# An average-pooling kernel that streams 134 MB through VectorE: merged output stores, one store kept back to the end, and a finer tail

## The chip, the cores and the metric

The kernel runs on one core of a Trainium2 chip. The metric is device time in microseconds (us), lower is better. Executions of one kernel mostly agree within about 0.3%, so the median of several is quoted. The "span" of a profile is the time from the first to the last instruction of the profiled execution; it is about 2 us shorter than the device time of the same execution.

## The reference

The input `x` has the shape 32 x 256 x 4096 in float32 (134 MB). Every 16 neighbouring values of a row are averaged, so the output is 32 x 256 x 256 (8.4 MB).

```python
def reference(x, output_size):          # output_size = 256
    for i in range(output_size):
        start = int(i * length / output_size)
        end = int((i + 1) * length / output_size)
        result[:, :, i] = np.mean(x[:, :, start:end], axis=-1)
    return result
```

## The kernel before

The whole input is one flat run, cut into tiles of 128 partitions x W columns. For each tile there is one load (issued from SyncE), one reduce over 16 columns on VectorE, one multiply by 1/16 on ScalarE, and one store (issued from ScalarE). There are 24 tiles of 8192 columns (4 MB, one contiguous row of 32 KB per partition), then ten of 4096 and twelve of 2048, so that little work is left after the last load.

```python
    tail = [4096] * 10 + [2048] * 12
    segs = [FULL] * nfull + tail                     # FULL = 8192, nfull = 24
    # ... cut ...
    loads = ctx.enter_context(tc.tile_pool(name="loads", bufs=5))
    outs = ctx.enter_context(tc.tile_pool(name="outs", bufs=10))
    for j, W in enumerate(segs):
        Wo = W // K                                  # K = 16
        # ... cut: x_tile [P, W] from loads, o_tile [P, Wo] from outs ...
        nc.sync.dma_start(out=x_tile,
            in_=xs[xoff:xoff + P * W].rearrange("(p w) -> p w", p=P))
        nc.vector.reduce_sum(out=o_tile,
            in_=x_tile.rearrange("p (o k) -> p o k", k=K), axis=mybir.AxisListType.X)
        nc.scalar.mul(out=o_tile, in_=o_tile, mul=inv_k)
        nc.scalar.dma_start(
            out=os[ooff:ooff + P * Wo].rearrange("(p w) -> p w", p=P), in_=o_tile)
```

Of the kernel before, what the change touches and what calls it, by code (L numbers as in the profile page):

```python
# [1 line left out]

# [4 lines left out]


@with_exitstack
def kernel(  # L10
    ctx: ExitStack,
    tc: tile.TileContext,
    x: bass.AP,
    output_size: int,
    out: bass.AP,
):
    nc = tc.nc
    fp32 = mybir.dt.float32

    B, C, L = x.shape  # L20
    Bo, Co, O = out.shape
    assert B == Bo and C == Co and O == output_size
    assert L % O == 0
    K = L // O

    P = nc.NUM_PARTITIONS

    total_cols = (B * C * L) // P
    FULL = 8192

    tail = [4096] * 10 + [2048] * 12
    nfull = (total_cols - sum(tail)) // FULL
    assert nfull * FULL + sum(tail) == total_cols
    segs = [FULL] * nfull + tail

    xs = x.rearrange("b c l -> (b c l)")
    os = out.rearrange("b c o -> (b c o)")

    inv_k = 1.0 / K

    loads = ctx.enter_context(tc.tile_pool(name="loads", bufs=5))
    outs = ctx.enter_context(tc.tile_pool(name="outs", bufs=10))

    xoff = 0
    ooff = 0
    for j, W in enumerate(segs):
        Wo = W // K
        x_tile = loads.tile([P, W], fp32, tag="x", padded_shape=[P, FULL])
        o_tile = outs.tile([P, Wo], fp32, tag="o", padded_shape=[P, FULL // K])
        nc.sync.dma_start(  # L50
            out=x_tile,
            in_=xs[xoff:xoff + P * W].rearrange("(p w) -> p w", p=P),
        )
        nc.vector.reduce_sum(  # L54
            out=o_tile,
            in_=x_tile.rearrange("p (o k) -> p o k", k=K),
            axis=mybir.AxisListType.X,
        )
        nc.scalar.mul(out=o_tile, in_=o_tile, mul=inv_k)  # L59
        nc.scalar.dma_start(  # L60
            out=os[ooff:ooff + P * Wo].rearrange("(p w) -> p w", p=P),
            in_=o_tile,
        )
        xoff += P * W
        ooff += P * Wo


# [1 line left out]
_INS = ['x', 'output_size']  # L69
_OUTS = [((32, 256, 256), 'float32')]  # L70
#: Inputs that are plain numbers.
_NUMBERS = {'output_size': 256}


# [26 lines left out]
```

## Time and profile before

| | before |
|---|---|
| time, median | 341.87 us (4 runs; 341.77 over 12) |
| span of the profiled run | 340.0 us |
| load packets on the 16 DMA engines (a packet is one row that one engine moves) | 1.76 to 334.30 us |
| last store packet ends | 338.60 us |
| VectorE busy | 279.4 us, 82% |

In all profile lines DVE is VectorE, ACT ScalarE, SP SyncE; SPq and ACTq are their DMA-issuing instructions; L54 is a line of the kernel. These are lines of the profile page of the kernel before: the DMA engines' busy tenths and the rate in 40 slices of the span, the two DMA queues (loads on q1, stores on q10), the chain that ended last, and the reduce.

```profile
span 340.0 us, 355 instructions
DMA  7999999999999999999999999999999999999993
GB/s 312 440 432 447 425 423 459 394 462 406 442 447 405 459 397 459 431 417 459 397 459 405 444 447 405 463 394 455 435 407 434 423 427 434 425 416 420 421 420 135
...
q1 hardware_dynamic: 6624, 134.22, 91.9%
q10 hardware_dynamic: 6624, 8.39, 6.7%
...
DMA 92%; DVE 5%; issue 1%; ACT 0%; SPq 0%; DVEq 0%
...
L54 DVE TENSOR_REDUCE o_tile<-x_tile 128x512 f32<-128x8192 f32 (+2 forms) x46 | 279.4, 6087 | 57.6 <-DMA x_tile<-in_x_dram 55.1
...
out_dram<-o_tile ACTq DMA_DIRECT2D x24, 256.0 KB, 15.0
```

The DMA engines are full from the second slice to the last but one, and the chain is nearly all load. VectorE has 60 us to spare.

The timeline of the end shows the chain: the last reduce, its multiply, its store (start us, duration us, engine, line, operation).

```profile
334.75 2.29 DVE L54 TENSOR_REDUCE o_tile<-x_tile 128x128 f32<-128x2048 f32 x1 [0.34 <-ACT o_tile L59]
337.07 0.31 ACT L59 ACTIVATE o_tile<-o_tile 128x128 f32<-128x128 f32 x1 [2.32 <-DVE o_tile L54]
337.41 0.34 ACTq L60 DMA_DIRECT2D out_dram<-o_tile  x1
```

### The profile page before, as it was taken

The page shows a single profiled execution, that of the slowest core. Times are in us where ns is not written, and L with a number is a line of the kernel's source. Part 1 is how long each engine was busy: PE and PEld are TensorE (multiplying, and loading weights), DVE is VectorE, ACT ScalarE, POOL GpSimd, SP SyncE. Part 2 cuts the span into 40 slices and gives each one's busy share as a digit, 9 for nine tenths or more (in the row PEclk, how much of TensorE's full clock was granted, in tenths as well). Part 3 has the DMA queues.
Part 4 walks back from the last instruction along what each step waited for, and adds up shares of the span by engine and source line. Part 5 has one row for each costly group of instructions (what it writes and reads, how often), then busy time and mean ns, then how long its engine had stood idle before and what let it go on. Part 6 is the DMA issues. An engine that isn't in the chain of part 4 may idle for free.

```text
span 340.0 us, 355 instructions
## 1 busy us (share of the span) xinstructions
DVE 279.4 (82%) x46; ACT 24.3 (7%) x47; POOL 0.2 (0%) x4
## 2 busy tenths in 40 slices
DVE  0488898888988788988888988889889998899885
ACT  1000000000000000000000000000001000001111
POOL 0000000000000000000000000000000000000000
DMA  7999999999999999999999999999999999999993
GB/s 312 440 432 447 425 423 459 394 462 406 442 447 405 459 397 459 431 417 459 397 459 405 444 447 405 463 394 455 435 407 434 423 427 434 425 416 420 421 420 135
DMA packets 13251, 142.64 MB, mean 420 GB/s; under 512 B 1472, under 2 KB 4288, under 8 KB 7360
## 3 DMA queue, kind: packets, MB, share of 16 engines
q1 hardware_dynamic: 6624, 134.22, 91.9%
q10 hardware_dynamic: 6624, 8.39, 6.7%
q14 instruction: 3, 0.02, 0.0%
HBM read 134.22 MB, written 8.39 MB: 419 GB/s over the span
## 4 chain that ended last, share of the span: by engine, by line
DMA 92%; DVE 5%; issue 1%; ACT 0%; SPq 0%; DVEq 0%
DMA x_tile<-in_x_dram 89%; DVE o_tile L54 5%; DMA out_dram<-o_tile 3%; ACT o_tile L59 0%; SPq L50 0%; DVEq L54 0%
## 5 line engine op out<-in xcount | busy, mean ns | idle before, releaser
L54 DVE TENSOR_REDUCE o_tile<-x_tile 128x512 f32<-128x8192 f32 (+2 forms) x46 | 279.4, 6087 | 57.6 <-DMA x_tile<-in_x_dram 55.1
L59 ACT ACTIVATE o_tile<-o_tile 128x512 f32<-128x512 f32 (+2 forms) x46 | 23.0, 500 | 312.4 <-DVE o_tile L54 307.8
L59 ACT ACT_TABLE_LOAD x1 | 1.3, 1283 | 0.7 <-PEq L82 0.7
L82 POOL MEMSET const-bfloat16-1.0<- 128x1 bf16 x1 | 0.1, 102 | 0.0
L82 POOL MEMSET const-uint8-127<- 128x1 uint8 x1 | 0.1, 101 | 0.0
L82 POOL MEMSET const-float32-0.0<- 128x1 f32 x1 | 0.1, 99 | 0.2 <-issue 0.2
L82 POOL MEMSET const-float32-1.0<- 128x1 f32 x1 | 0.1, 98 | 0.0
## 6 DMA issues: line engine op xcount, KB each, us to landing
x_tile<-in_x_dram SPq DMA_DIRECT2D x24, 4096.0 KB, 41.2
x_tile<-in_x_dram SPq DMA_DIRECT2D x10, 2048.0 KB, 20.4
x_tile<-in_x_dram SPq DMA_DIRECT2D x12, 1024.0 KB, 10.4
out_dram<-o_tile ACTq DMA_DIRECT2D x24, 256.0 KB, 15.0
out_dram<-o_tile ACTq DMA_DIRECT2D x10, 128.0 KB, 11.6
out_dram<-o_tile ACTq DMA_DIRECT2D x12, 64.0 KB, 8.2
```

The costliest lines, as they stand in the source:

```text
L54: nc.vector.reduce_sum(out=o_tile, in_=x_tile.rearrange("p (o k) -> p o k", k=K), axis=mybir.AxisListType.X,)
L59: nc.scalar.mul(out=o_tile, in_=o_tile, mul=inv_k)
L82: nc = _bacc.Bacc("TRN2", target_bir_lowering=False, num_devices=1)
```

## The change

The intent is to store in fewer, larger DMAs, issued later (eight tiles after the last tile of a group), and to shorten what is left after the last load. Four or five neighbouring tiles share one output tile and one store (three and one at the very end); the group of the last four full tiles is "deferred": its 1 MB store is issued from SyncE after the last load. The tail ends in four tiles of 1024 columns with load buffers of their own, and the last multiply is done by VectorE. There are four big load buffers in place of five.

```diff
-    tail = [4096] * 10 + [2048] * 12
+    tail = [(10, 4096, 5), (10, 2048, 5), (4, 1024, 3)]    # tiles, columns, tiles per store
+    plan = [(nfull, FULL, 4)] + tail
 ... (cut: the list of groups)
+    STORE_DELAY = 8
+    defer_first_segs = {nfull - 4}
+    for gi, gr in enumerate(groups):
+        last = gr["segs"][-1]
+        if gr["segs"][0] in defer_first_segs and gr["W"] == FULL:
+            gr["kind"] = "defer"
+        elif gi == final_group:
+            gr["kind"] = "final"
+        elif last + STORE_DELAY >= nseg_total:
+            gr["kind"] = "late"
+        else:
+            gr["kind"] = "sync"
+            gr["store_at"] = last + STORE_DELAY
-    loads = ctx.enter_context(tc.tile_pool(name="loads", bufs=5))
-    outs = ctx.enter_context(tc.tile_pool(name="outs", bufs=10))
+    loads = ctx.enter_context(tc.tile_pool(name="loads", bufs=4))
+    outs = ctx.enter_context(tc.tile_pool(name="outs", bufs=4))
+    small = ctx.enter_context(tc.tile_pool(name="small", bufs=4))
+    keep = ctx.enter_context(tc.tile_pool(name="keep", bufs=max(1, len(defer_first_segs))))
 ... (cut: views of a group in HBM, "(s p w) -> p s w", and in its output tile)
-        nc.scalar.mul(out=o_tile, in_=o_tile, mul=inv_k)
-        nc.scalar.dma_start(out=os[...], in_=o_tile)
+        if not final_seg:
+            nc.scalar.mul(...)                             # on the tile's slice of the group
+        else:
+            nc.vector.tensor_scalar_mul(...)
+            nc.scalar.dma_start(out=hbm_ap(gi), in_=sbuf_ap(gi))
+        if gr["kind"] == "late" and s == gr["segs"][-1]:
+            nc.scalar.dma_start(out=hbm_ap(gi), in_=sbuf_ap(gi))
+        for gi2 in stores_at.get(s, []):
+            nc.scalar.dma_start(out=hbm_ap(gi2), in_=sbuf_ap(gi2))
+    for gi, gr in enumerate(groups):
+        if gr["kind"] == "defer":
+            nc.sync.dma_start(out=hbm_ap(gi), in_=sbuf_ap(gi))
```

More of the change, by code (lines that the diff above doesn't have):

```diff
@@ L29 @@
     FULL = 8192
-    tail = [4096] * 10 + [2048] * 12
-    nfull = (total_cols - sum(tail)) // FULL
-    assert nfull * FULL + sum(tail) == total_cols
-    segs = [FULL] * nfull + tail
+    tail = [(10, 4096, 5), (10, 2048, 5), (4, 1024, 3)]
+    tail_cols = sum(n * w for n, w, _ in tail)
+    nfull = (total_cols - tail_cols) // FULL
+    assert nfull * FULL + tail_cols == total_cols
+    plan = [(nfull, FULL, 4)] + tail
     xs = x.rearrange("b c l -> (b c l)")
@@ L39 @@
     inv_k = 1.0 / K
-    loads = ctx.enter_context(tc.tile_pool(name="loads", bufs=5))
-    outs = ctx.enter_context(tc.tile_pool(name="outs", bufs=10))
-    xoff = 0
+    seg_w = []
+    for (nseg, W, G) in plan:
+        seg_w += [W] * nseg
+    nseg_total = len(seg_w)
+    seg_xoff = []
+    off = 0
+    for W in seg_w:
+        seg_xoff.append(off)
+        off += P * W
+    groups = []
     ooff = 0
-    for j, W in enumerate(segs):
+    seg = 0
+    for (nseg, W, G) in plan:
         Wo = W // K
-        x_tile = loads.tile([P, W], fp32, tag="x", padded_shape=[P, FULL])
-        o_tile = outs.tile([P, Wo], fp32, tag="o", padded_shape=[P, FULL // K])
+        for j0 in range(0, nseg, G):
+            g = min(G, nseg - j0)
+            groups.append({
+                "W": W, "Wo": Wo, "og": ooff + j0 * P * Wo,
+                "segs": list(range(seg, seg + g)),
+            })
+            seg += g
+        ooff += nseg * P * Wo
@@ new lines @@
+    group_of_seg = {}
+    j_in_group = {}
+    for gi, gr in enumerate(groups):
+        for k, s in enumerate(gr["segs"]):
+            group_of_seg[s] = gi
+            j_in_group[s] = k
+    final_group = len(groups) - 1
+    assert len(groups[final_group]["segs"]) == 1
+    STORE_DELAY = 8
[11 more added lines that the diff above has]
+            gr["store_at"] = last + STORE_DELAY
@@ new lines, with hbm_ap @@
+    stores_at = {}
+    for gi, gr in enumerate(groups):
+        if gr["kind"] == "sync":
+            stores_at.setdefault(gr["store_at"], []).append(gi)
+    loads = ctx.enter_context(tc.tile_pool(name="loads", bufs=4))
+    outs = ctx.enter_context(tc.tile_pool(name="outs", bufs=4))
+    small = ctx.enter_context(tc.tile_pool(name="small", bufs=4))
+    keep = ctx.enter_context(tc.tile_pool(name="keep", bufs=max(1, len(defer_first_segs))))
+    group_tiles = {}
+    def hbm_ap(gi, lo=0, hi=None):
+        gr = groups[gi]
+        Wo = gr["Wo"]
+        g = len(gr["segs"])
+        if hi is None:
+            hi = g
+        n = hi - lo
+        base = gr["og"] + lo * P * Wo
+        if n == 1:
+            return os[base:base + P * Wo].rearrange("(p w) -> p w", p=P)
+        return os[base:base + n * P * Wo].rearrange("(s p w) -> p s w", p=P, w=Wo)
@@ new lines, in sbuf_ap @@
+    def sbuf_ap(gi, lo=0, hi=None):
+        gr = groups[gi]
+        Wo = gr["Wo"]
+        g = len(gr["segs"])
+        if hi is None:
+            hi = g
+        t = group_tiles[gi][:, lo * Wo:hi * Wo]
+        if hi - lo == 1:
+            return t
+        return t.rearrange("p (s w) -> p s w", w=Wo)
+    for s in range(nseg_total):
+        W = seg_w[s]
+        Wo = W // K
+        gi = group_of_seg[s]
+        gr = groups[gi]
+        j = j_in_group[s]
+        g = len(gr["segs"])
+        final_seg = s == nseg_total - 1
+        if j == 0:
+            pool = keep if gr["kind"] == "defer" else outs
+            tag = "keep" if gr["kind"] == "defer" else "o"
+            group_tiles[gi] = pool.tile([P, g * Wo], fp32, tag=tag, name="ot",
+                                        padded_shape=[P, 4 * (FULL // K)])
+        o_tile = group_tiles[gi]
+        if W == 1024:
+            x_tile = small.tile([P, W], fp32, tag="xs")
+        else:
+            x_tile = loads.tile([P, W], fp32, tag="x", padded_shape=[P, FULL])
@@ L50 @@
         nc.sync.dma_start(
             out=x_tile,
-            in_=xs[xoff:xoff + P * W].rearrange("(p w) -> p w", p=P),
+            in_=xs[seg_xoff[s]:seg_xoff[s] + P * W].rearrange("(p w) -> p w", p=P),
         )
         nc.vector.reduce_sum(
-            out=o_tile,
+            out=o_tile[:, j * Wo:(j + 1) * Wo],
             in_=x_tile.rearrange("p (o k) -> p o k", k=K),
@@ L58 @@
         )
-        nc.scalar.mul(out=o_tile, in_=o_tile, mul=inv_k)
-        nc.scalar.dma_start(
-            out=os[ooff:ooff + P * Wo].rearrange("(p w) -> p w", p=P),
-            in_=o_tile,
-        )
-        xoff += P * W
-        ooff += P * Wo
+        if not final_seg:
+            nc.scalar.mul(
+                out=o_tile[:, j * Wo:(j + 1) * Wo],
+                in_=o_tile[:, j * Wo:(j + 1) * Wo],
+                mul=inv_k,
+            )
+        else:
+            nc.vector.tensor_scalar_mul(
+                out=o_tile[:, j * Wo:(j + 1) * Wo],
+                in0=o_tile[:, j * Wo:(j + 1) * Wo],
+                scalar1=inv_k,
+            )
+            nc.scalar.dma_start(out=hbm_ap(gi), in_=sbuf_ap(gi))
[3 more added lines that the diff above has]
+            nc.scalar.dma_start(out=hbm_ap(gi2), in_=sbuf_ap(gi2))
+    for gi, gr in enumerate(groups):
+        if gr["kind"] == "defer":
+            nc.sync.dma_start(out=hbm_ap(gi), in_=sbuf_ap(gi))
 _INS = ['x', 'output_size']
```

## The prediction

> **What bounds the kernel now.** The 16 DMA engines. The page's DMA row shows nine tenths or more in all but the end slices; the queue table gives loads 91.9% and stores 6.7% of 16 engines' span of 340.0 us. The chain of waits is 89% load, 5% reduce, 3% store. VectorE is busy 82% and waits 55.1 us for loads.
>
> The trace's packet records cost a packet by its size alone: loads 1213 ns (32 KB), 611 (16 KB), 309 (8 KB); stores 84 ns (2 KB), 46 (1 KB), 27 (512 B); completion writes 9 ns. Summed over 16 engines: 335.3 us, between the first load packet at 1.8 us and the last store packet at 338.6. A 32 KB packet in 1213 ns is 432 GB/s over 16 engines, at the 435 GB/s fabric ceiling that the Trainium skill states ("DMA: Bandwidth & Descriptors", Specifications). So only 1.5 us of engine time is idle, nearly all of it after the last load packet (334.3): reduce 2.29, multiply 0.31, store issue and data about 1.6, then 1.35 to the end.
>
> **What the change does.** Loads: same bytes; 2 of the 2048-column loads become 4 of 1024. At an estimated 159 ns per 4 KB packet, +0.1 us. Stores: the merged store of 4 or 5 tiles keeps the same contiguous runs (2 KB, 1 KB, 512 B), so the same packets, +0.15 us for the 256 B ones, and some 31 fewer completion writes, -0.3 us. DMA work stays about 335.3 us.
>
> The gain is in the tail alone: the 1 MB store kept back (32 packets x 84 ns = 2.7 us per engine) and late stores fill the DMA time while the last tile is reduced. That tile's reduce halves to about 1.2 us (estimate from 2.29) and its multiply moves to VectorE. The last load should land about 2.5 us earlier (332), and then about 5.3 us of stores remain.
>
> **What it costs.** Stores alternate with load packets one for one: the first store's packets are 1.30 us apart (1213 + 84), as the skill says of round-robin by packet (same page, "Queues, rings and completion order"). A merged store of 32 packets should thus take four loads, about 43 us, instead of 15. Consequences: (a) the first reduce of the fifth store group waits about 3 us for its output buffer, harmless; (b) loads and stores share eight completion semaphores in turn (seen in the trace), so a load can be held back by a store eight issues earlier; 2 to 3 loads are still queued then, so at most 1 to 2 us near the end; (c) the last reduce reuses the buffer of a 640 KB store that ends about when the last load does, so it waits some 2 us in the tail. Four load buffers instead of five: a load is issued when a reduce ends, with over two loads (20 us) still queued.
>
> **Prediction.** Span 338.7 us, time 340.5 us: -0.4%, within 2%. Range 338.8 to 343.5.
>
> **What would show it.** Total packet time unchanged within 1 us; store issue-to-landing about 40 us for merged stores; last load landing near 332; store queue busy after it for 4 to 6 us; the last reduce waiting for a store, not for its load; no DMA slice below nine tenths in mid-run.
>
> **What would make it wrong.** Upward: semaphore sharing or an output buffer starving loads for several us (a dip in mid-run), or stores piling up after the last load. Downward: merged rows move as larger packets, saving up to about 8 ns of each of some 5,900 store packets, 3 us per engine (estimate from 84 against 46 ns).
>
> Chances: faster by over 2% 0.02, within 2% 0.93, slower by over 2% 0.05.

## More of the kernel before

Where a run is shown by windows, the columns are the window, its length, busy time of VectorE, ScalarE and GpSimd, a clock that doesn't matter here, the mean busy share of the 16 DMA engines, and GB/s.

```profile
15.00:250.00 235.00, 197.76 (x24) 14.47 (x23) 0.00 (x0) 1.00 1.00 430
250.00:300.00 50.00, 46.54 (x10) 3.96 (x9) 0.00 (x0) 1.00 1.01 428
300.00:330.00 30.00, 26.76 (x12) 3.62 (x11) 0.00 (x0) 1.00 1.02 419
...
334.30:338.60 4.30, 2.40 (x2) 0.62 (x2) 0.00 (x0) 1.00 0.12 33
338.60:340.00 1.40, 0.00 (x0) 0.00 (x0) 0.00 (x0) 1.00 0.00 0
```

Two things are to be seen. First, the busy share goes over 1.00, so packet records overlap: those up to the last load packet add up to 334.8 us per engine in a stretch of 332.5 us. Second, between the last load packet (334.30) and the last store packet (338.60) the DMA engines are only 12% busy. Of those 4.30 us, 0.88 x 4.30 = 3.8 us are idle.

## The result, and the profile after

| | before | change |
|---|---|---|
| time, median | 341.77 us (12 runs, 341.54 to 342.16) | 338.32 us (9 runs, 338.13 to 339.53) |
| ratio | | 0.9902, 95% interval 0.9892 to 0.9911 |
| span, profiled run | 340.0 us | 337.7 us, the slowest of the nine |
| span, the other eight | | 336.3 to 336.8 us |

A ratio is the mean time of one kernel's fast runs over that of the other's fast runs of the same rounds, so it is not quite the ratio of the medians quoted. The change is 1.0% faster, 3.45 us, where I predicted 0.4% (about 1.4 us); 338.32 us lies just below my range of 338.8 to 343.5.

The profile page of the change (the profiled run was one of its rare slow ones, see below) answers the lines shown of before: span, DMA busy tenths, queues, chain, and the merged stores with their size and the time from issue to landing.

```profile
span 337.7 us, 266 instructions
DMA  8999999999999999999999999999999999999997
...
q1 hardware_dynamic: 7440, 135.27, 93.5%
q10 hardware_dynamic: 5808, 7.34, 6.0%
...
DMA 77%; DVE 20%; issue 2%; ACT 0%; SPq 0%; DVEq 0%
...
out_dram<-ot ACTq DMA_DIRECT2D x5, 1024.0 KB, 42.2
...
out_dram<-ot SPq DMA_DIRECT2D x1, 1024.0 KB, 6.6
```

The packets are as many in sum (13251 before, 13250 after), and the middle of the run has the same rate. The merged 1 MB stores took 42.2 us to land instead of 15.0, as predicted. SyncE does wait for stores before it issues some loads (7 times, 63.5 us in sum; 6 times and 51.5 us before), but other loads are queued then and no slice of mid-run falls below nine tenths. The last slice went from 3 to 7 tenths: the gain is in the tail.

The change (run again2): a usual execution. Its windows are to be laid beside those of before.

```profile
15.00:250.00 235.00, 199.89 (x24) 14.47 (x23) 0.00 (x0) 1.00 1.00 431
250.00:300.00 50.00, 47.28 (x11) 4.38 (x10) 0.00 (x0) 1.00 1.01 428
300.00:328.00 28.00, 24.85 (x11) 3.20 (x10) 0.00 (x0) 1.00 1.02 419
...
331.20:335.20 4.00, 2.07 (x3) 0.26 (x1) 0.00 (x0) 1.00 0.94 315
335.20:336.60 1.40, 0.00 (x0) 0.00 (x0) 0.00 (x0) 1.00 0.00 0
```

The first three rows differ by at most 1 GB/s from those of before. The last load packet now ends at 331.17 instead of 334.30, and the 4 us after it, in which the last tile is still reduced and stored, are 94% busy instead of 12%. The gain in span is 340.0 - 336.6 = 3.4 us: the last load ends 3.1 us earlier, and the stretch after it is 0.3 us shorter.

One part of the change does nothing at all. These lines of the timeline of the change show the fourth multiply and the first merged store.

```profile
50.83 0.63 ACT L154 ACTIVATE ot<-ot 128x512 f32<-128x512 f32 x1 [9.08 <-DVE ot L148]
51.49 0.42 ACTq L171 DMA_DIRECT2D out_dram<-ot  x1
```

The store goes out as soon as its group is complete, not eight tiles later: the framework's scheduler sets the order, not the place in the source. I built the kernel with delays of 0, 1 and 8 tiles as well and compared the instruction order of every engine: it is the same in all three, so there was nothing to run. (The three programs differ in the numbers of buffer names alone.) So "issued later" must not enter any explanation of the result, and it had entered my prediction.

### The profile page after: what moved, and what is told of

Read it like the earlier page. It is cut to its first block, busy times and chain, and to the rows that moved or that the text cites. A ratio compares the mean times of both kernels' runs of the same rounds, so it can differ in the third digit from the quotient of the medians.

```text
span 337.7 us, 266 instructions
## 1 busy us (share of the span) xinstructions
DVE 279.4 (83%) x49; ACT 24.4 (7%) x48; POOL 0.2 (0%) x4
## 2 busy tenths in 40 slices
DMA packets 13250, 142.63 MB, mean 422 GB/s; under 512 B 1472, under 2 KB 4032, under 8 KB 7616
## 4 chain that ended last, share of the span: by engine, by line
DMA 77%; DVE 20%; issue 2%; ACT 0%; SPq 0%; DVEq 0%
DMA x_tile<-in_x_dram 48%; DMA out_dram<-ot 29%; DVE ot L148 20%; ACT ot L154 0%; SPq L144 0%; DVE ot L160 0%; DVEq L148 0%
## 5 line engine op out<-in xcount | busy, mean ns | idle before, releaser
L148 DVE TENSOR_REDUCE ot<-x_tile 128x512 f32<-128x8192 f32 (+3 forms) x48 | 279.2, 5839 | 55.7 <-DMA x_tile<-in_x_dram 55.7
L154 ACT ACTIVATE ot<-ot 128x512 f32<-128x512 f32 (+3 forms) x47 | 23.1, 492 | 306.9 <-DVE ot L148 306.9
## 6 DMA issues: line engine op xcount, KB each, us to landing
out_dram<-ot ACTq DMA_DIRECT2D x5, 1024.0 KB, 42.2
```

What stands on the lines that cost most here:

```text
L148: nc.vector.reduce_sum(out=o_tile[:, j * Wo:(j + 1) * Wo], in_=x_tile.rearrange("p (o k) -> p o k", k=K), axis=mybir.AxisListType.X,)
L154: nc.scalar.mul(out=o_tile[:, j * Wo:(j + 1) * Wo], in_=o_tile[:, j * Wo:(j + 1) * Wo], mul=inv_k,)
```

## The experiments

Three theories were to be told apart. Theory 1: the gain is idle DMA time after the last load, filled by the kept-back store. Theory 2: the merging of the stores saves DMA or issue time. Theory 3: the shorter chain after the last load (smaller last tile, multiply on VectorE). All times of one round are beside runs of the kernel before on the same chip: 341.82 us in the first round (9 runs), 341.75 in the second (11), 341.83 in the third (9). All outputs were correct.

### b_keep4: only the kept-back store

The kernel before, and nothing else of the change:

```diff
+        held = nfull - 4 <= j < nfull
+        o_tile = kept[:, k0:k0 + Wo] if held else outs.tile(...)
 ...
-        nc.scalar.dma_start(out=os[...], in_=o_tile)
+        if not held:
+            nc.scalar.dma_start(out=os[...], in_=o_tile)
 ... after the loop
+    nc.sync.dma_start(out=os[...].rearrange("(s p w) -> p s w", p=P, w=Wk),
+                      in_=kept.rearrange("p (s w) -> p s w", w=Wk))
```

> The kernel before, with one part of the change alone: the outputs of the last four full tiles are kept back and stored in one 1 MB store after the last load, on the load queue; every other store as it was. Theory 1 (idle tail): before, the DMA engines are idle for about 3.9 us after the last load packet (334.3 us), which my prediction missed because the packet records overlap by 1 to 2%; 32 packets x 84 ns = 2.7 us of store work moved there make the last load land about 2.6 us earlier (near 331.7) and the run about 2.5 us shorter: 339.3 us. Theory 2 (merging): only one merged store here, so nearly nothing is gained: 341.5 us. Theory 3 (shorter tail chain): the chain after the last load is as before: 341.8 us.

Measured: 339.10 us (338.95 to 339.19), ratio 0.992 (0.9906 to 0.9933); span 337.2 us. The windows of the end:

```profile
328.00:331.60 3.60, 3.27 (x2) 0.31 (x1) 0.00 (x0) 1.00 0.99 398
331.60:336.00 4.40, 2.47 (x2) 0.62 (x2) 0.00 (x0) 1.00 0.70 253
```

The last load packet ends at 331.64, which is 2.66 us earlier than before; the work moved is 32 packets x 84 ns = 2.69 us. The stretch after it is as long as before but 70% busy. This one edit gives 2.7 us of the 3.45. Theory 1 holds, with its number. The kept-back store is also merged and stands on SyncE's queue behind the loads; keeping it back on ScalarE's queue was not tried.

### b_tail: only the finer tail

```diff
-    tail = [4096] * 10 + [2048] * 12
+    tail = [4096] * 10 + [2048] * 10 + [1024] * 4
 ...
-        nc.scalar.mul(out=o_tile, in_=o_tile, mul=inv_k)
+        if j < len(segs) - 1:
+            nc.scalar.mul(out=o_tile, in_=o_tile, mul=inv_k)
+        else:
+            nc.vector.tensor_scalar_mul(out=o_tile, in0=o_tile, scalar1=inv_k)
```

> The kernel before, with the tail of the change alone: two of the 2048-column tiles become four of 1024, and the last multiply is on VectorE. DMA work is the same. Theory 3 (shorter tail chain): from the last load packet to the end it was 5.7 us before and 4.5 us in the profile of the change, so about 1.1 us are gained: 340.7 us. Theories 1 and 2 as the only cause: 341.8 us.

Measured: 341.54 us (341.50 to 341.86), ratio 0.9994 (0.998 to 1.0008): nothing clear of noise. The windows of its end, and the last store and load in its chain of waits:

```profile
332.50:334.00 1.50, 1.50 (x3) 0.26 (x1) 0.00 (x0) 1.00 0.78 279
...
335.60:339.80 4.20, 1.42 (x2) 0.00 (x0) 0.00 (x0) 1.00 0.09 19
```

```profile
324.27 7.11 DMA out_dram<-o_tile
...
331.46 3.74 DMA x_tile<-in_x_dram
```

The stretch after the last load did shrink, from 5.7 to 4.2 us. But the last load packet ends at 335.55 instead of 334.30, since the last load was issued only at 331.46, when a store that had been issued at 324.27 had landed; the DMA engines ran partly dry (0.78) meanwhile. In the trace, loads and stores take eight completion semaphores (counters by which a DMA reports that it has landed) in turn, and a DMA may be issued only when the one eight places before it has landed. Halving the tiles halves the work that eight DMAs hold in flight. So a finer tail by itself is paid for with a late last load. The small tiles' own load buffers, which this run lacks and the change has, are not the wait seen here: the semaphores are.

### b_merge: only the merged stores and the four load buffers

The change with its tail, kept-back store and last multiply put back to those of before:

```diff
-    tail = [(10, 4096, 5), (10, 2048, 5), (4, 1024, 3)]
+    tail = [(10, 4096, 5), (11, 2048, 5), (1, 2048, 1)]
-    defer_first_segs = {nfull - 4}
+    defer_first_segs = set()
-            nc.vector.tensor_scalar_mul(...)
+            nc.scalar.mul(...)
```

> The kernel before, with the merging and delaying of the stores and the four load buffers of the change, but nothing kept back and the tail tiles as before. Theory 2 (fewer, larger stores save DMA time or issue time): faster by 2 us or more, 339.5 us. Theories 1 and 3: packets are the same, so 341.8 us within 0.5; if anything slower, as the late stores pile up after the last load.

Measured: 341.07 us (340.84 to 341.50), ratio 0.9981 (0.9969 to 0.9994): 0.75 us faster. Theory 2 as the main cause is out (it wanted 2 us or more), and my 341.8 was a little too high. The last load packet ends 0.55 us earlier than before (333.75). Fewer completion writes (34 DMAs less, 9 ns each on every engine) would account for 0.3 us of it; the rest I did not trace further. Merging and four load buffers were changed together here, so only their sum is known to do no harm.

### nodefer: the change without the kept-back store

```diff
-    defer_first_segs = {nfull - 4}
+    defer_first_segs = set()
```

> The change without the kept-back store: that group of four is stored 8 tiles after its last like the others. Theory 1: it loses the 2.5 us and keeps the shorter tail chain: about 340.7 us. Theory 2: it merges one store more than the change: 338.3 us or less. Theory 3: as the change, 338.3 us.

Measured: 340.33 us (340.25 to 340.74), ratio 0.9959. Without its kept-back store the change keeps 1.5 of its 3.45 us. Against b_merge, which differs by the tail, its buffers and the last multiply, it is 0.74 us faster: that is what Theory 3 is worth where the loads are not held. Against the change, the kept-back store is worth 2.0 us on top of the other parts, less than alone.

### b_keep8: keep back twice as much

As b_keep4 with eight tiles kept back (2 MB; the output pool is 6 deep for want of room).

```diff
-    NK = 4
+    NK = 8
```

> As b_keep4, with the outputs of eight full tiles kept back (2 MB, 5.4 us of store work per engine) in place of four. Theory 1: the idle DMA time after the last load was 3.9 us, so the gain ends there: the last load packet ends near 329.0 us, but the kept-back store then outlasts the reduce of the last tile, and the run ends about 1.4 us after the last store packet at about 334.7: span near 336.1, time 338.0 us, 1.1 us faster than b_keep4, not 2.7. Rival (whatever is kept back is free): 336.4 us.

Measured: 338.43 us (338.28 to 338.53), ratio 0.9902. The windows of its end:

```profile
329.10:335.20 6.10, 2.45 (x2) 0.62 (x2) 0.00 (x0) 1.00 0.95 355
```

The first megabyte kept back brought 2.7 us, the second only 0.7. The last load ends at 329.13, but now the stores after it fill 6.1 us at 95%: the idle time is used up. This puts what can be taken from the idle time at 3.4 us, and it rules out that keeping back is free without limit. A kernel with five load buffers, the old tail and, but for the kept-back one, one output store per tile is as fast as the change.

### again, again2, again3: the change once more

The kernel is the change, unaltered.

> The change unaltered, once more, for a second trace: its profiled run (span 337.7 us) was the slowest of its nine, the other eight had spans of 336.3 to 336.8 us. Theory 1 takes the usual span for 336.4: the loads and stores fill the DMA engines from 1.76 us to the last store. If the usual trace still shows the last load issued only when the merged store of the tiles 34 to 38 has landed (329.1 us, 8 us late), but with less idle DMA time around it, that wait is not what makes the profiled run slower; if the load is issued well before the queue runs dry, it is. Time 338.3 us.

> The change unaltered, to catch a trace of a usual run (span 336.3 to 336.8 us) beside the two slow ones that I have (337.7 and 338.0). In both slow ones the last load is issued after the store of the tiles 39 to 43 (329.1 after 328.7, 329.4 after 328.8) and its first packet moves 2 us later, at 331.1, behind that store's packets, with 0.5 us of idle DMA time in between. If the trace is of a usual run, the theory that this order costs the 1.3 us expects the last load to be issued before that store, or its packets to follow at about 1 us; the rival expects the same order and the time lost elsewhere. If the trace is slow again, nothing new.

> As again2, a second look for a usual run's trace: the same two theories, and the same numbers of each.

Measured: again 338.39 us (338.10 to 340.39, six runs, two of them at 339.89 and 340.39; the profiled one is the former); again2 338.40 and again3 338.45 us, one run each, spans 336.6. So there are traces of both kinds. In the slow execution first shown, the chain of waits of the change contains:

```profile
315.40 13.69 DMA out_dram<-ot
329.09 0.02 issue
329.11 4.42 DMA x_tile<-in_x_dram
```

The last load is the eighth DMA after the merged store of tiles 34 to 38 and waits until that store has landed at 329.09 us. In the usual execution (again2) the same wait exists, but it ends earlier, as the timeline from 300 us on shows (eleven loads issued between 302.95 and 327.18 us, then the kept-back store, then the store of tiles 39 to 43):

```profile
302.95 24.23 SPq L144 DMA_DIRECT2D x_tile<-in_x_dram  x11
...
327.28 0.40 SPq L175 DMA_DIRECT2D out_dram<-ot  x1
...
328.94 0.38 ACTq L168 DMA_DIRECT2D out_dram<-ot  x1
```

There the last load goes out at 326.9 us (in again3 at 324.1), while the loads before it still run until about 329.2. In both usual traces it goes out before the store of tiles 39 to 43, in both slow ones (the second is again's) after it. The store that it waits for took 13.7 and 13.6 us to land in the slow traces, 10.9 and 8.5 in the usual ones; why was not traced. The windows between 328 and 331.2 us tell what it makes, first for the slow execution, then for again2:

```profile
328.00:331.20 3.20, 3.20 (x4) 0.82 (x3) 0.00 (x0) 1.00 0.83 254
```

```profile
328.00:331.20 3.20, 3.20 (x4) 0.82 (x3) 0.00 (x0) 1.00 1.02 405
```

So the same wait costs nothing while there are loads in the queue, and over 1 us when it ends after they have run out (spans of 337.7, 338.0 and 338.6 us in the three slow executions, the last without a trace, against 336.6). In the first of them 0.17 x 3.20 = 0.5 us of the 1.1 us are idle engines. In addition, the 512 B store packets take 2.57 us in the sum of an engine, against 2.16 in again2: 0.4 us. Long 4 KB packets of the late load add less than 0.1 us: 7 of its 128 last over 200 ns, up to 641, and in again2 2 do, up to 628.

### lanefree and lanefree2: the last load behind another semaphore

The store of tiles 39 to 43 is cut in two, so that the last load is the eighth DMA after an early load.

```diff
         if gr["kind"] == "late" and s == gr["segs"][-1]:
-            nc.scalar.dma_start(out=hbm_ap(gi), in_=sbuf_ap(gi))
+            cuts = [0, 3, 5] if W == 2048 else [0, g]
+            for lo, hi in zip(cuts, cuts[1:]):
+                nc.scalar.dma_start(out=hbm_ap(gi, lo, hi), in_=sbuf_ap(gi, lo, hi))
```

> The change with one edit: the store of the tiles 39 to 43 is cut in two, so that the last load is the eighth DMA after a load, no longer after the merged store of the tiles 34 to 38, and doesn't share its completion semaphore. In the profile of the change the last load was held for 8 us by it, and the kept-back store behind it; DMA engines were idle for about 0.5 us then. Theory 1 (what counts is idle DMA time): the last load is issued near 321 us; 0.5 to 1 us faster than the slowest run of the change, and 0 to 0.5 us faster than its median: 338.0 us. Rival (the hold costs its full length on the chain): 4 us or more faster.

> lanefree once more, for the spread: the change had 3 of 15 runs between 339.5 and 340.4 us and the others at 338.1 to 338.6. If the held last load makes those slow runs, none of the four to six here is above 338.8 us (lanefree: 338.38 to 338.57 in four). If chance of the chip makes them, about one in five is.

Measured: 338.46 us (338.38 to 338.57) and 338.23 us (337.98 to 338.30), ratios 0.9902 and 0.9893. The last load went out at 322.2 us in the profiled run of lanefree. None of eight runs is above 338.57 us, while 3 of 17 of the change were above 339.5. The median didn't move: a hold of 8 us on one load is not 8 us, nor 4, of time. That the hold makes the slow runs is what the traces of two of them and of two usual ones say, and best below agrees; no experiment shows it. That the edit removes them is likely, but eight runs are few (with 3 in 17 they would be without a slow one about once in five times).

### rows: the same bytes in fewer, larger store packets

Within a group each partition owns one contiguous run, so a merged store has one row of 8 KB per partition in place of four of 2 KB.

```diff
-            in_=xs[seg_xoff[s]:seg_xoff[s] + P * W].rearrange("(p w) -> p w", p=P),
+            in_=xs[seg_xoff[gr["segs"][0]]:seg_xoff[gr["segs"][0]] + g * P * W]
+                .rearrange("(p w) -> p w", p=P)[:, j * W:(j + 1) * W],
 ...
-        return os[base:base + n * P * Wo].rearrange("(s p w) -> p s w", p=P, w=Wo)
+        return os[base:base + n * P * Wo].rearrange("(p w) -> p w", p=P)
```

> The change with another assignment of the data to partitions: within a group of 4 or 5 tiles each partition owns one contiguous run, cut in columns, so that a merged store has one contiguous run of 8, 5 or 2.5 KB per partition instead of 4 or 5 of 2, 1 or 0.5 KB. Loads have the same packets (32, 16, 8, 4 KB), only farther apart. Theory 1 with the packet times of the trace (309 ns for 8 KB against 4 x 84; about 198 for 5 KB against 5 x 46, about 103 for 2.5 KB against 5 x 27, both estimates on that line): 1.3 + 0.5 + 0.5 = 2.3 us less DMA work per engine; the merged store lands after about 13 us instead of 42, as 8 of its packets alternate with 8 of the load's: 336.2 us. Rival (bytes alone count, or the larger strides of the loads slow them): 338.3 us or more.

Measured: 338.45 us (338.27 to 338.61), ratio 0.9902: no gain. 8642 packets move what 13250 did, the 1 MB stores land after 16.1 us instead of 42.2, and the summed packet times fall by 1.1 us against again2 (334.4 against 335.5). The store packets save more than twice that, but the load packets, now farther apart in memory, become longer by over 1 us in the sum. The time does not follow even the 1.1 us that are left. The windows of its end say where some of it went:

```profile
331.50:335.20 3.70, 2.41 (x3) 0.51 (x2) 0.00 (x0) 1.00 0.81 319
```

The stretch after the last load is 0.7 us idle, against 0.2 in again2. The effects are not separated here; what is shown is that a saving in summed packet times did not become time.

### best: fewer small tiles

An attempt to beat both kernels: lanefree, with 4 MB moved from the 2048-column tiles to 4096-column ones (four tiles of 1 MB become two of 2 MB; the 8 MB of my expectation are a slip), which run at a better rate (428 against 419 GB/s).

```diff
-    tail = [(10, 4096, 5), (10, 2048, 5), (4, 1024, 3)]
+    tail = [(12, 4096, 4), (6, 2048, 3), (4, 1024, 3)]
-            cuts = [0, 3, 5] if W == 2048 else [0, g]
+            cuts = [0, 2, 3] if W == 2048 else [0, g]
```

> lanefree with fewer small tiles: 12 of 4096 columns, 6 of 2048 and 4 of 1024 in place of 10, 10 and 4. The DMA rate is 431.5 GB/s in the stage of the 32 KB rows, 428.5 in that of 16 KB and 420 in that of 8 KB, so some 8 MB moved from 8 KB to 16 KB rows gain 0.3 to 0.4 us if nothing else changes: 338.1 us. Theory 1 says that no version of this design gets below about 337.8, since bytes at these rates, 1.75 us of start and 1.4 us of end add up to a span of 336.0 us. VectorE may be later at the end with larger tiles, which would eat the gain: 338.4.

Measured: 341.43 us (340.87 to 341.72), ratio 0.9988: all of the gain is gone, and neither side of my expectation had it. Its chain of waits, and the window around it:

```profile
314.13 13.65 DMA out_dram<-ot
327.78 0.01 issue
327.80 0.33 SPq L144
```

```profile
327.00:329.00 2.00, 2.00 (x2) 0.31 (x1) 0.00 (x0) 1.00 0.41 111
```

Here the first of the last three loads waits for the merged store of the last 4096-column group until 327.8 us, the other two stand behind it in SyncE's order, and no other load is left: the DMA engines are 41% busy for 2 us (1.2 us lost), and the late loads' 4 KB packets average 215 ns over all four loads instead of 159 (sum 6.87 us against 5.09 in lanefree: 1.8 us). Together that is about the 2.9 us by which its span (339.5) exceeds that of the change (336.6). The held load of the change is thus a near miss of a real loss. Why late 4 KB packets get longer was not tested.

## Why the prediction was wrong

What stood the test:
- The kernel is bound by the DMA engines; packets, bytes and rates in the middle did not change (431 and 428 against 430 and 428 GB/s).
- "Fewer completion writes, -0.3 us" was of the right kind, though it was not isolated: b_merge, all in all, is 0.75 us faster.
- "The gain is in the tail alone", in the main: of 3.45 us, 2.7 come from keeping back one store (b_keep4), 0.75 from merging and four buffers, 0.3 to 0.7 from the finer tail. They don't add up, since the idle time can be used only once.
- Merged stores land after about 42 us (I said 43), as store and load packets alternate.
- The last load would end near 332, about 2.5 us earlier: 331.17 in the usual run, of which b_keep4 shows 2.66 us; the other 0.5 us I had not counted on.

The step that failed is this one: "So only 1.5 us of engine time is idle, nearly all of it after the last load packet". I took 335.3 us of summed packet times from the 336.8 us between the first and last packet. But packet records overlap (334.8 us of them in 332.5 us, up to the last load), so the sum is larger than the time in which engines are busy. The window after the last load shows 3.8 us idle, and b_keep8 shows by experiment that 2.7 + 0.7 = 3.4 us can be taken from it. The change takes 3.4 us of span. The mechanism was right; the term was less than half its size. With 3.8 in place of 1.5, the same sum would have given a gain of up to 3.8 us and a time near 338.

That error hid behind a second: I let "about 5.3 us of stores remain" after the last load, so that 332 + 5.3 + 1.4 = 338.7 us looked sound. In again2 it is 331.2 + 4.0 + 1.4 = 336.6 us: 1.3 MB remain (3.8 us of packet times), which fit into the 4.0 us that the last tile needs anyway. The 2.1 us between the two spans are, within 0.2 us, the 3.8 - 1.5 = 2.3 us that the idle term lacked. The 5.3 us came from taking `STORE_DELAY` at its word; the delay isn't in the program that runs.

For the same reason cost (c) did not occur: the last reduce waits for its load alone, since the store whose buffer it takes was issued eight tiles earlier than I had it. Cost (a) didn't occur either. VectorE's waits in the change name no other releaser than loads:

```profile
DVE ot L148 <- DMA x_tile<-in_x_dram: 55.7, 35, 13.0
```

Cost (b), a load held by a store eight issues earlier, is real: no time in most executions, 1.1 to 2.0 us of span in the slow ones (two of the three traced), about 2.9 us in best. The way down that I named, larger packets, was the wrong one: merged rows keep their packets, and larger ones (rows) bring nothing.

What stays open: 0.45 of the 0.75 us of b_merge, why late 4 KB packets last longer, and why the store that holds the last load lands late in some executions. The change is not clearly beaten by a variant: the change, b_keep8, both lanefree runs and rows all lie between 338.2 and 338.5 us. This is about the floor of the design, as an estimate from the traces: 1.75 us before the first packet, 142.6 MB at the 429 GB/s that again2 shows up to its last load (332.4 us), and 1.4 us after the last packet make 335.6 us of span; the change has 336.6. What lanefree may have over the change is a narrower spread.

## What to carry to other kernels

In a kernel that is bound by DMA, look for DMA time that nothing uses: the stretch after the last load, in which the last tile is still computed, can take stores that were kept back, as much as fits and no more. Measure that stretch as a window of the profile, and don't take it as the rest of a sum of packet times, whose records may overlap. Before you reason about where a DMA is issued, read in the trace where it is issued, and ask of each late load which earlier DMA shares its completion semaphore: here a hold was free while other loads were queued (again2) and cost time once they had run out (best).

## What the Trainium skill lacked or had wrong

- "DMA: Bandwidth & Descriptors", Bandwidth: its warning says without a condition that for HBM to SBUF the HBM side binds at about 358 GB/s. A note above it limits that figure to both cores of a pair streaming, and its own 16 MB row has 425 GB/s with the pair's other core idle. Here one core moved 430 GB/s for 235 us, loads and stores mixed, so the warning, read by itself, would have misled; the page's fabric ceiling of 435 GB/s was the nearer bound.
- The same page, "Queues, rings and completion order", has an engine switch between queues after a packet of typically 9 to 17 descriptors. Here the switch came after every recorded packet, one row each: store packets 1.30 us apart between loads of 1213 ns, and 42.2 us for a store with 32 packets per engine. Whether the profile's packet is the page's packet or its descriptor is not shown.
- No page that I read gives the rate by row size for a mix of loads and stores: 430 to 431 GB/s with load rows of 32 KB, 428 with 16 KB, 419 with 8 KB.
- No page that I read says that packet records overlap, so that a busy share can reach 1.02 and summed packet times exceed busy time (here by 2.2 us up to the last load).
- No page that I read says that loads and stores take eight completion semaphores in turn under this framework, which held one load for 8 us in the change; best, where three loads were held, had a span 2.9 us longer.
